# Convolution and gate columns as seven half products, and a 31-tap convolution by even and odd tokens

## The chip, the cores and the metric

The kernel runs on one core of one Trainium2 chip. The metric is the time of one execution on the device in microseconds (us), lower is better; the number that counts is the median of several executions. Beside it stands one execution taken with the hardware profiler, whose span runs from its first instruction to its last.

## The reference

One hybrid decoder block over 2048 tokens with a model width of 1024, all in float32. What the change touches is the first half of it:

```python
h = rms_norm(x, norm_w) * (1 + scale) + shift          # 2048 x 1024
z = h @ w_in                                           # one projection, 10240 columns
a, b, g_conv, q, k, v, g_attn, m_conv, m_attn = split(z)
u = a * sigmoid(b)                                     # 1024 channels
u = depthwise_causal_conv(u, conv_w, conv_b)           # 31 taps over the tokens
u = silu(layer_norm(u)) * silu(g_conv);  y_conv = u @ w_conv_out
...                                                    # attention: 12 heads in 3 dilation groups
y_attn = (o * silu(g_attn)) @ w_attn_out
y = sigmoid(m_conv) * y_conv + sigmoid(m_attn) * y_attn
out = x + gate * (y @ w_out)
```

a, b, g_conv, m_conv and m_attn are 1024 columns each of the projection: five of its ten thousand-column blocks.

## The kernel before, in words

**Number format.** Every float32 factor of a matmul is split into a high part (`hi`, `wh`: a copy by ScalarE, written ACT in the profile) and a low part (`lo`, `wl`: the factor less its high part, one subtraction on VectorE, written DVE, or on GpSimd, written POOL). A product is then three matmuls: high by high, high by low and low by high. One product of a 128-column block with 512 tokens over the 1024 rows of the model width is 8 x 3 = 24 matmuls of 128x512.

**Stages, by the time in the profiled execution.** Up to about 45 us the modulation vector, rotary tables and first loads. Then twelve units, one for each attention head (46 to 1086 us): the query, key and value columns of a head are projected for all 16 token blocks, and the blocks of the head before are attended to. During the first unit h is made (`h_first`, `h_part`): transposes on TensorE, `hf` by VectorE from PSUM (two buffers), the high part by ACT, the low part by VectorE or POOL; from then on `hT_hi` and `hT_lo` stay in SBUF, 2048 tokens each. From 1086 to 1191 us the three groups' attention is merged and multiplied by its gate (`merge_step`, two halves of the heads, 16 token blocks each, matmuls on line 350 into `pzg`). From 1193 to 2064 us runs the **channel stage**, and after it the output part: `ya` (attention output projection), the layer norm of the convolution, `yc`, and the last projection, up to the end at 2525 us.

**The channel stage.** `jobs` alternates `ab_block` and `gate_blocks` over eight blocks of 128 channels. `ab_block` computes the b column and the a column of its block for four tiles of 512 tokens (`z_chan`, 24 matmuls each on line 806), forms u with a tanh on ACT and one VectorE instruction (line 822), and puts the 31 taps of the convolution on a list (`conv_todo`): each tap is one VectorE instruction over 1024 tokens (line 835, accumulating in the SBUF tile `ca`), two of them per tap. `gate_blocks` computes three columns of a block (g_conv, m_conv, m_attn), passes them through ACT (line 864; for g_conv also line 866 on VectorE) and stores them. After each tile `run_conv` takes three to six taps from the list and issues them. Weights of the next job are loaded and split while a job runs (`load_w`, lines 316 to 329).

**What sets the order.** Within an engine's queue instructions run in the order in which they stand. TensorE's order is written out by hand in the units, the merges and the output part, and left to the framework's scheduler in the channel stage; for the other engines the scheduler decides, with a few instructions pinned. Nearly all transfers are issued by one queue, SP. A tile that is reused waits until its last reader and its last transfer are done. Before the last four tiles of the stage `beside()` calls `start_output`, which closes the convolution's pool and loads and splits w_attn_out (lines 894 to 896) in its place; the ai tiles (the attention's gated output) and the d tiles (the convolution's result, read back from DRAM) follow.

## Time and profile before

| | |
|---|---|
| median of 3 runs | 2528.01 us (2527.86 to 2530.43) |
| profiled execution | 2527.02 us, span 2525.2 us |
| granted TensorE clock, mean | 0.997 |
| TensorE (PE) busy | 2491.1 us, 99% of the span |
| VectorE (DVE) busy | 1668.0 us, 66% |
| ScalarE (ACT) busy | 756.7 us, 30% |
| GpSimd (POOL) busy | 252.7 us, 10% |
| DMA | 278.51 MB, mean 110 GB/s |

Busy times are sums over the whole span, so a share is a mean over stages with different limits; what a change in one stage is worth is read from that stage. In the groups of a view, `out<-in` are the names of the tiles that an instruction writes and reads, `x480` a count, and the time after the second bar the idle time of its engine ahead of it, with what ended that. In the timeline the first number is the start in us from the span's start and the second the duration; a row with `x2` holds two instructions. A matmul's own duration overlaps that of the next, so the pitch of TensorE's work is read from starts.

### The profile page before, as it was taken

To read this page: it belongs to the slowest core of one execution; us is meant where nothing else is said; L and a number is where in the kernel's file an instruction comes from. 1 tells how busy PE (TensorE), PEld (TensorE's weight loads), DVE (VectorE), ACT (ScalarE), POOL (GpSimd) and SP (SyncE) were. 2 spreads that over 40 slices of the span, in tenths; PEclk is the share of its full clock that TensorE was granted. 3 is DMA by queue.
4 is the path that set the end of the run, shared out by engine and by line. 5 is a ranking of instruction groups with operands and counts; after the bars stand their busy time and mean duration, and the time that the engine had idled before them with its cause. 6 is when DMAs were issued, how large, how long until landed. Compare 5 with 4: busy or idle time off the path is not lost.

```text
span 2525.2 us, 38211 instructions
## 1 busy us (share of the span) xinstructions
PE 2491.1 (99%) x13361; PEld 2222.6 (88%) x13361; DVE 1668.0 (66%) x3528; ACT 756.7 (30%) x2366; POOL 252.7 (10%) x503
## 2 busy tenths in 40 slices
...
GB/s 234 117 107 116 155 109 99 101 117 119 115 73 54 57 36 38 51 132 148 41 48 70 64 80 83 39 70 60 63 64 70 95 148 324 295 221 231 124 135 111
DMA packets 262653, 278.51 MB, mean 110 GB/s; under 512 B 25464, under 2 KB 195736, under 8 KB 262462
## 3 DMA queue, kind: packets, MB, share of 16 engines
...
HBM read 175.12 MB, written 100.86 MB: 109 GB/s over the span
## 4 chain that ended last, share of the span: by engine, by line
PE 95%; DVE 1%; ACT 1%; DMA 1%; POOL 1%; issue 0%; SPq 0%; POOLq 0%; ACTq 0%; DVEq 0%
PE pz L350 31%; PE pg L806 21%; PE yc L948 7%; PE out L948 7%; PE pb L806 7%; PE pa L806 7%; PE ya L948 3%; PE pzg L350 3%; PE ps L422 3%; PE po L441 3%; PE ptq L412 2%; PE ptp L433 1%; DMA pos_i<-in_positions_dram 0%; DVE tab L164 0%; PE pt_x L258 0%; DMA raw_u<-in_w_in_dram 0%
## 5 line engine op out<-in xcount | busy, mean ns | idle before, releaser
L835 DVE SCALAR_TENSOR_TENSOR ca<-up,chan,ca 128x1024 f32<-128x1024 f32 x480 | 593.9, 1286 | 3.6
L350 PE MATMUL pz<-wh_u,hT_lo 128*128 128x384 f32 x1536 | 536.3, 350 | 1.3 <-POOL hT_lo L271 1.2
L350 PE MATMUL pz<-wh_u,hT_hi 128*128 128x384 f32 x1536 | 518.3, 337 | 5.6 <-ACT wh_u L326 2.7
L350 PE MATMUL pz<-wl_u,hT_hi 128*128 128x384 f32 x1536 | 519.3, 338 | 0.3 <-DVE wl_u L329 0.2
L378 DVE SCALAR_TENSOR_TENSOR qk<-pz,st,wqk 128x128 f32<-128x128 f32 x384 | 117.0, 347 | 335.3 <-POOL st L107 335.3
L806 PE MATMUL pg<-hT_hi,wh_gm 128*128 128x512 f32 x768 | 298.6, 389 | 0.0
L806 PE MATMUL pg<-hT_lo,wh_gm 128*128 128x512 f32 x768 | 298.6, 389 | 0.0
L806 PE MATMUL pg<-hT_hi,wl_gm 128*128 128x512 f32 x768 | 297.9, 389 | 0.0
L350 PEld LDWEIGHTS pz<-wh_u,hT_hi 128*128 128x128 f32 x1536 | 290.5, 189 | 7.8 <-ACT wh_u L326 3.3
L350 PEld LDWEIGHTS pz<-wh_u,hT_lo 128*128 128x128 f32 x1536 | 289.2, 188 | 3.2 <-POOL hT_lo L271 1.5
L350 PEld LDWEIGHTS pz<-wl_u,hT_hi 128*128 128x128 f32 x1536 | 289.6, 189 | 2.1 <-DVE wl_u L329 1.6
L414 ACT ACTIVATE qkT<-ptq 128x256 f32<-128x256 f32 x192 | 73.8, 384 | 420.2 <-PE ptq L412 419.7
L864 ACT ACTIVATE gt<-pg 128x512 f32<-128x512 f32 x96 | 57.1, 597 | 421.4 <-PE pg L806 417.1
L806 PEld LDWEIGHTS pg<-hT_hi,wl_gm 128*128 128x128 f32 x768 | 144.2, 188 | 30.0
L806 PEld LDWEIGHTS pg<-hT_lo,wh_gm 128*128 128x128 f32 x768 | 144.2, 188 | 30.0
L806 PEld LDWEIGHTS pg<-hT_hi,wh_gm 128*128 128x128 f32 x768 | 144.2, 188 | 29.7
L107 POOL TENSOR_TENSOR st<-st,mhalf 128x2 f32<-128x2 f32 x192 | 136.5, 711 | 16.0
L367 ACT ACTIVATE sq<-pz 128x128 bf16<-128x128 f32 x384 | 106.2, 277 | 97.4 <-PE pz L350 90.3
L106 POOL TENSOR_SCALAR st<-st 128x2 f32<-128x2 f32 x192 | 45.6, 237 | 813.9 <-ACT sq L367 813.9
L427 ACT ACTIVATE sm<-sm,osb 128x128 f32<-128x128 f32 (+1 forms) x192 | 88.7, 462 | 62.3 <-DVE osb L425 59.0
L806 PE MATMUL pb<-hT_hi,wh_ab 128*128 128x512 f32 x256 | 99.7, 389 | 0.0
L806 PE MATMUL pb<-hT_lo,wh_ab 128*128 128x512 f32 x256 | 99.6, 389 | 0.0
...
## 6 DMA issues: line engine op xcount, KB each, us to landing
qkv_d<-qkv SPq DMA_DIRECT2D x128, 192.0 KB, 2.2
...
lqk<-qkv_d SPq DMA_DIRECT2D x128, 128.0 KB, 2.2
...
wada<-in_w_ada_dram SPq DMA_DIRECT2D x16, 512.0 KB, 8.2
lv<-qkv_d SPq DMA_DIRECT2D x128, 64.0 KB, 1.8
raw_ab<-in_w_in_dram SPq DMA_DIRECT2D x64, 128.0 KB, 2.2
```

The lines of the kernel that those rows point to most:

```text
L107: nc.gpsimd.tensor_tensor(dst, scratch[:, :n], mhalf[:, :n], op=ALU.pow)
L350: nc.tensor.matmul(pz[:, :width], a[:, k, P * j : P * j + P], w[:, :width], start=(m == 0), stop=(m == 23))
L367: nc.scalar.activation(sq, pz[:, P * i : P * i + P], AF.Square, scale=1.0 / math.sqrt(P), accum_out=st[:, i : i + 1])
L378: nc.vector.scalar_tensor_tensor(qk[:, 2 * i : 2 * i + 2].rearrange("p a b -> p (a b)"), pz[:, P * i : P * i + P], st[:, 2 + i : 3 + i], w ...
L414: nc.scalar.activation(qkT.rearrange("p a b -> p (a b)"), pt[:, :256], AF.Copy)
L422: nc.tensor.matmul(ps[:, P * i : P * i + P], box["q"][:, 0, :], kt[:, 1, :], start=True, stop=True)
L427: nc.scalar.activation(sm[:, :w], sm[:, :w], AF.Exp, scale=-1.0, bias=o[:, P : P + 1], accum_out=o[:, P + 1 : P + 2])
L441: nc.tensor.matmul(po[:, :P], box["pT"][:, P * i : P * i + P], vt, start=(i == 0), stop=(i == nk - 1))
L806: nc.tensor.matmul(pz, w[k][:, P * col : P * col + P], a[:, k, 512 * t : 512 * t + 512], start=(m == 0), stop=(m == 23))
L835: nc.vector.scalar_tensor_tensor(accs[c], up[:, t0 + i : t0 + i + 1024], chan[:, cb, i : i + 1], accs[c], op0=ALU.mult, op1=ALU.add)
L864: nc.scalar.activation(th, pz, AF.Tanh, scale=0.5)
L948: nc.tensor.matmul(pz, w, xx, start=(m == 0), stop=(m == len(terms) - 1))
```

## The change

**Products of halves.** The projection of the five blocks is cut in two along the tokens (two halves of 1024), the tokens of a half in two tiles of 512, the model width in two halves of 512, and the columns into pairs of 128. The two-by-two product of such quarters is done by Strassen's scheme (Winograd's form) with seven products of quarters where there were eight: `quad` runs them in the order of `PRODUCTS`, 12 matmuls each. It needs sums of quarters on both sides. Those of h (S1 to S4) are made once: h is also written to DRAM while it is made (`h_d`), VectorE forms the sums during units 4 to 10 (`quarter_load`, `quarter_sum`, kept in `s_d`), and `quarter_place` loads and splits them into the tiles of h that are no longer needed, for half 0 during the merges (whose token blocks come in another order for it), for half 1 during the last quad of half 0. Those of the weights (T1 to T4) are made per quad by POOL (`column_steps`), one quad ahead, and each of the seven weight quarters is split by ACT and by VectorE (3) or POOL (4). The sums of products run through PSUM accumulation, ACT copies (`kept`) and three additions per quad, two on VectorE and one on POOL.

**Order.** There are 40 quads, 20 per half: 8 of a and b columns, 12 of gate columns. Half 0 is done for all channels before half 1. TensorE's order is now written by hand in this stage too. After each product `after` issues one step of the next quad's weights and three or four steps of the convolution. The g_conv gate uses Silu on ACT.

**Convolution.** For each half and channel block the 31 taps are done on 512 even and 512 odd tokens: u is stored apart for even and odd tokens (`ut`), and three short filters of 16, 15 and 16 taps run over the even, the odd and the summed tokens (`both`, one POOL addition), accumulating in PSUM, with one joining step between (`conv_parts`). The last 15 values go from half 0 to half 1 by `tail` and `odd_tail`. The convolution's list is emptied before the last quad, and `start_output` stands there.

Where instructions moved, first VectorE in the middle of the channel stage. Before, in a gate block: `ca` are the two accumulators of a channel block in SBUF, `up` is u, `gt` a gate tile.

```order
L835 SCALAR_TENSOR_TENSOR ca_0_17319<-up_16743,chan,ca_0_17319 128x1024 [waits DVE_49]
L866 SCALAR_TENSOR_TENSOR gt_0_2_17120<-gt_0_2_17120,pg_0_2_17095 128x512 [waits Activation_49]
L835 SCALAR_TENSOR_TENSOR ca_1_17321<-up_16743,chan,ca_1_17321 128x1024 [waits DVE_49]
L846 TENSOR_TENSOR usum<-usum,ca_1_16651 128x1024 [waits DVE_49]
L835 SCALAR_TENSOR_TENSOR ca_0_17319<-up_16743,chan,ca_0_17319 128x1024 [waits DVE_49]
```

After, around the start of a block's convolution: `ce` is an accumulator in PSUM (L998 even tokens, L1027 the summed tokens of the block before), L919 a split of a weight quarter for the next quad, L962 and L976 additions of products, L1060 forms u. Behind them on the queue everything waits that they wait for.

```order
L976 TENSOR_TENSOR spare_hi<-spare_hi,pcab_6_18368 128x512 [waits PE_49]
L1027 SCALAR_TENSOR_TENSOR ce_5_18053<-us_5_18010,pair_taps,ce_5_18053 128x512 [waits DVE_49] x2
L1060 SCALAR_TENSOR_TENSOR ut_6_18364<-spare_hi 128x2x256 [waits Activation_49]
L1027 SCALAR_TENSOR_TENSOR ce_5_18053<-us_5_18010,pair_taps,ce_5_18053 128x512 [waits DVE_49]
L1060 SCALAR_TENSOR_TENSOR ut_6_18364<-spare_hi,paab_6_18366 128x2x256 [waits PE_49]
L919 TENSOR_TENSOR slB_896_18544<-wB_896_18535,shB_896_18543 128x512 [waits DMAHW0_49,Activation_49]
L1027 SCALAR_TENSOR_TENSOR ce_5_18053<-us_5_18010,pair_taps,ce_5_18053 128x512 [waits DVE_49]
L995 TENSOR_SCALAR ce_6_18514<-ut_6_18364,chan 128x512 [waits DVE_49]
L1027 SCALAR_TENSOR_TENSOR ce_5_18053<-us_5_18010,pair_taps,ce_5_18053 128x512 [waits DVE_49]
L998 SCALAR_TENSOR_TENSOR ce_6_18514<-ut_6_18364,chan,ce_6_18514 128x512 [waits DVE_49]
```

Fewer elements per instruction, more instructions, and the weight splits and product sums stand between the taps.

Next SP, the queue of transfers, at the end of the stage. Before, the w_attn_out loads (`fraw`, two at a time) stand among the stores of the last gate block (`gt`), ahead of all loads of ai:

```order
L867 DMA g_d<-gt_0_0_21116 128x512 [waits DMAHW3_49,DVE_49]
L894 DMA fraw<-in_w_attn_out_dram 128x512 [waits DMAHW4_49,Pool_49]
L894 DMA fraw<-in_w_attn_out_dram 128x512 [waits DMAHW5_49,PE_49]
L894 DMA fraw<-in_w_attn_out_dram 128x512 [waits DMAHW6_49,DMAHW4_49,DVE_49]
L894 DMA fraw<-in_w_attn_out_dram 128x512 [waits DMAHW7_49,DMAHW5_49,DVE_49]
L867 DMA g_d<-gt_0_1_21151 128x512 [waits DMAHW0_49,DVE_49]
```

After, behind the last store of the last quad (`gt_6`), the loads of ai, eight loads of d and the last store of the convolution; the first d waits for TensorE:

```order
L1073 DMA ma_d<-gt_6_22782 128x512 [waits DMAHW7_49,Activation_49]
L1098 DMA fraw<-ai_d 128x512 [waits DMAHW0_49]
L1098 DMA airaw<-ai_d 128x512 [waits DMAHW1_49]
L1279 DMA ma_0_22832<-ma_d 128x512 [waits DMAHW2_49]
L1187 DMA d_22841<-u_d 128x2x512 [waits DMAHW3_49,PE_49]
...
L1034 DMA u_d<-ca_7_22535 128x1024 [waits DMAHW1_49,DVE_49]
...
L1187 DMA d_23071<-u_d 128x2x512 [waits DMAHW0_49]
L1224 DMA gg_0_23350<-g_d 128x512 [waits DMAHW1_49]
...
L1098 DMA fraw<-in_w_attn_out_dram 128x512 [waits DMAHW5_49]
L1098 DMA fraw<-in_w_attn_out_dram 128x512 [waits DMAHW6_49]
```

So these loads moved from inside the stage to behind its end.

Last ACT at the change of halves: L832 takes over a placed quarter for half 1 (A or S), L955 is a `kept` copy, `paab_0` the bank of half 1's first quad, L918 a weight's high part.

```order
L832 ACTIVATE S_hi_19404<-spare_hi 128x512 [waits DMAHW3_49]
L832 ACTIVATE A_hi_19438<-landing_19447 128x512 [waits DMAHW4_49]
L832 ACTIVATE A_hi_19438<-landing_19451 128x512 [waits DMAHW5_49]
L955 ACTIVATE spare_hi<-paab_0_19457 128x512 [waits PE_49,Pool_49]
L918 ACTIVATE shT_2048_19521<-wT_2048_19519 128x512 [waits PE_49,Pool_49]
L918 ACTIVATE shT_2048_19538<-wB_2048_19473 128x512 [waits PE_49]
L955 ACTIVATE spare_hi<-paab_0_19457 128x512 [waits DVE_49,PE_49]
```

All 28 placings stand ahead of half 1's first copy out of PSUM; before, nothing of this kind was there.

The diff, cut to its core:

```diff
@@ -261,15 +276,16 @@
     def h_first(kk, pt):
         for a in range(2):
             k = 2 * kk + a
-            last = nc.scalar.activation(hi[:, k, :256], pt[:, 256 * a : 256 * a + 256], AF.Identity,
+            last = nc.scalar.activation(part(hi, k, 0, 256), pt[:, 256 * a : 256 * a + 256], AF.Identity,
                                  scale=mod[:, KC + k : KC + k + 1], bias=mod[:, k : k + 1])
         for a in range(2):
             k = 2 * kk + a
             hf = xp.tile([P, 2, 256], F32, tag="hf", name=f"hf0_{k}", bufs=2)
             nc.vector.tensor_scalar(hf[:, 0], pt[:, 256 * a : 256 * a + 256], mod[:, KC + k : KC + k + 1],
                                     mod[:, k : k + 1], op0=ALU.mult, op1=ALU.add)
-            (nc.gpsimd if a else nc.vector).tensor_tensor(lo[:, k, :256], hf[:, 0], hi[:, k, :256].bitcast(F32),
+            (nc.gpsimd if a else nc.vector).tensor_tensor(part(lo, k, 0, 256), hf[:, 0], part(hi, k, 0, 256).bitcast(F32),
                                                           op=ALU.subtract)
+            nc.sync.dma_start(h_d[k, :, :256], hf[:, 0])
...
+        nc.sync.dma_start(h_d[2 * kk : 2 * kk + 2, :, P * j : P * j + 256].rearrange("a p t -> p a t"), hf)
...
+    def quarter_sum(half, k, n, dst, x0, x1, op):
+        q = [aside["sq", name] for name in (dst, x0, x1)]
+        tc.keep_in_program_order(nc.vector.tensor_tensor(*q, op=op))
+        nc.sync.dma_start(s_d[half, n - 1, k], q[0])
...
+    PRODUCTS = (("A11", "B11"), ("A12", "B21"), ("S2", "T2"), ("S1", "T1"), ("S3", "T3"), ("S4", "B22"), ("A22", "T4"))
...
+    def quarter_place(half, name, k, cols, raw, eng):
+        if k == 0 and cols.start == 0:
+            quarter_new(half, name)
+        h, l = (x[:, k, cols] for x in quarters[name])
+        nc.sync.dma_start(raw, quarter_src(half, name, k)[:, cols])
+        nc.scalar.activation(h, raw, AF.Copy)
+        eng.tensor_tensor(l, raw, h.bitcast(F32), op=ALU.subtract)
+
+    placing = [(n, k, c) for n in ("S2", "S3", "S4", "S1") for k in range(4) for c in (0, 256)]
...
+            if half == 1 and at_j >= 8:
+                for i, (n, k, c0) in enumerate(placing[4 * (at_j - 8) : 4 * (at_j - 8) + 4]):
+                    raw = wp.tile([P, 384], F32, tag="raw", name=f"raw{n}_{k}_{c0}", bufs=3)[:, :256]
+                    quarter_place(0, n, k, slice(c0, c0 + 256), raw, nc.gpsimd if i % 2 else nc.vector)
...
+    def column_steps(c0, c1):
+
+        q, got = {}, []
+
+        def load(name, kh, c):
+            t = q[name] = wr.tile([P, 4, P], F32, tag="wr", name=f"w{name}_{c0}")
+            nc.sync.dma_start(t, w_in[512 * kh : 512 * kh + 512, c : c + P].rearrange("(k p) c -> p k c", p=P))
+
+        def combine(name, dst, x0, x1):
+            if dst is None:
+                dst = wr.tile([P, 4, P], F32, tag="wr", name=f"w{name}_{c0}")
+            nc.gpsimd.tensor_tensor(dst, x0, x1, op=ALU.subtract)
+            q[name] = dst
+
+        def split(name, eng):
+            h, l = (ws.tile([P, 4, P], F32R, tag=f"s{hl}", name=f"s{hl}{name}_{c0}") for hl in "hl")
+            nc.scalar.activation(h, q[name], AF.Copy)
+            eng.tensor_tensor(l, q[name], h.bitcast(F32), op=ALU.subtract)
+            got.append((h, l))
+
+        def step(n):
+            if n == 0:
+                load("B11", 0, c0)
+                load("B21", 1, c0)
+                load("B12", 0, c1)
+                load("B22", 1, c1)
+            if n == 2:
+                combine("T1", q["B11"], q["B12"], q["B11"])
+                combine("T2", None, q["B22"], q["T1"])
+            if n == 4:
+                combine("T3", q["B12"], q["B22"], q["B12"])
+            if n == 6:
+                combine("T4", q["B21"], q["B21"], q["T2"])
+            split(PRODUCTS[n][1], nc.vector if n in (0, 3, 5) else nc.gpsimd)
+
+        return got, [lambda n=n: step(n) for n in range(7)]
...
+    def quad(name, got, sink, after):
+
+        pa, pb, pc = bank("z", f"pa{name}"), bank("s", f"pb{name}"), bank("o", f"pc{name}")
+        first = set()
+
+        def product(n, ps, more=False):
+            ah, al = quarters[PRODUCTS[n][0]]
+            wh, wl = got.pop(0)
+            terms = [t for k in range(4) for t in ((wh[:, k], ah[:, k]), (wh[:, k], al[:, k]), (wl[:, k], ah[:, k]))]
+            for m, (w, x) in enumerate(terms):
+                nc.tensor.matmul(ps, w, x, start=(m == 0 and ps.name not in first), stop=(m == 11 and not more),
+                                 skip_group_check=True)
+            first.add(ps.name)
+
+        def kept(ps):
+            t = scratch()
+            nc.scalar.activation(t, ps, AF.Copy)
+            return t
+
+        product(0, pa, True)
+        s1 = kept(pa)
+        after(0)
+        product(1, pb)
+        nc.vector.tensor_tensor(s1, s1, pb, op=ALU.add)
+        sink(0, 0, s1)
+        after(1)
+        product(2, pa, True)
+        s2 = kept(pa)
+        after(2)
+        product(3, pc, True)
+        s5 = kept(pc)
+        after(3)
+        product(4, pa, True)
+        s3 = kept(pa)
+        nc.gpsimd.tensor_tensor(s3, s3, s5, op=ALU.add)
+        after(4)
+        product(5, pc)
+        nc.vector.tensor_tensor(s2, s2, pc, op=ALU.add)
+        sink(0, 1, s2)
+        sink(1, 1, s3)
+        after(5)
+        product(6, pa)
+        sink(1, 0, pa)
+        after(6)
...
+        def odd(j):
+            def f():
+                w = chan[:, cb, 2 * j + 1 : 2 * j + 2]
+                if j == 0:
+                    box["o"] = bank("t", f"cq{half}_{cb}")
+                    nc.vector.tensor_scalar(box["o"], o[:, 2:514], w, None, op0=ALU.mult)
+                else:
+                    psum_o = box["o"]
+                    if j == HT - 1:
+                        box["o"] = cv.tile([P, 512], F32, tag="co", name=f"co{half}_{cb}")
+                    stt(box["o"], o[:, 2 + j : 514 + j], w, psum_o, op0=ALU.mult, op1=ALU.add)
+            return f
...
+        def join():
+            y = box["y"] = cv.tile([P, 512, 2], F32, tag="ca", name=f"ca{half}_{cb}")
+            nc.vector.tensor_add(y[:, 1:, 0], box["e"][:, 1:], box["o"][:, :511])
+            if half == 0:
+                nc.vector.tensor_copy(y[:, 0:1, 0], box["e"][:, 0:1])
+                nc.vector.tensor_copy(odd_tail[:, cb : cb + 1], box["o"][:, 511:])
+            else:
+                nc.vector.tensor_add(y[:, 0:1, 0], box["e"][:, 0:1], odd_tail[:, cb : cb + 1])
+            stt(box["e"], box["e"], pair_taps[:, cb, HT + 1 : HT + 2], box["o"], op0=ALU.subtract, op1=ALU.add)
...
+        def mixed(j):
+            def f():
+                dst = box["y"][:, :, 1] if j == HT else box["e"]
+                stt(dst, both[:, 1 + j : 513 + j], pair_taps[:, cb, j : j + 1], box["e"], op0=ALU.mult,
+                    op1=ALU.subtract if j == 0 else ALU.add)
+            return f
...
+        nc.gpsimd.tensor_add(both[:, 1:], e[:, 1:], o[:, 1:])
+        if half == 0:
+            nc.gpsimd.tensor_copy(tail[:, cb], ut[:, :, 513:528])
+        return [*[even(j) for j in range(HT + 1)], *[odd(j) for j in range(HT)], join,
+                *[mixed(j) for j in range(HT + 1)], done]
...
+    got, steps = job_columns(0)
+    for f in steps:
+        f()
+    for i, (kind, half, g, cb) in enumerate(jobs):
+        last_of_half = i + 1 < len(jobs) and jobs[i + 1][1] > half
+        nxt, steps = job_columns(i + 1) if i + 1 < len(jobs) else ([], [])
+        if i + 1 == len(jobs):
+            run_conv(len(conv_todo))
+            wraw_c.__exit__(None, None, None)
+            start_output()
+
+        def after(n):
+            if steps:
+                steps[n]()
+            if last_of_half:
+                name = PRODUCTS[n][0]
+                for k in range(4):
+                    quarter_place(1, name, k, slice(0, 512), landing(4 * n + k), nc.gpsimd if k % 2 else nc.vector)
+            else:
+                run_conv(3 if n < 5 else 4)
+
+        if kind is ab_quad:
+            ab_quad(half, cb, got, after)
         else:
-            job(cb, per, wts, start_output)
+            gate_quad(half, g[1], g[2], cb, got, after)
+        got = nxt
```

213 lines of the change are left out of this document (125 added, 88 removed).

## The prediction

> **What bounds the kernel now.** I read the page's busy line and its chain of waits first, then the busy time by stretches of the span.
>
> ```profile
> PE 2491.1 (99%) x13361; PEld 2222.6 (88%) x13361; DVE 1668.0 (66%) x3528; ACT 756.7 (30%) x2366; POOL 252.7 (10%) x503
> PE 95%; DVE 1%; ACT 1%; DMA 1%; POOL 1%; issue 0%; SPq 0%; POOLq 0%; ACTq 0%; DVEq 0%
> core 0: us, PE busy (x) PEld busy (x) DVE busy (x) ACT busy (x) POOL busy (x), PEclk, DMA share, GB/s
> 140.00:1010.00 870.00, 868.49 (x5554) 862.83 (x5555) 474.18 (x1766) 340.94 (x1412) 150.15 (x324) 1.00 0.31 92
> 1215.00:2075.00 860.00, 856.23 (x3771) 707.52 (x3770) 712.19 (x704) 134.24 (x254) 0.74 (x6) 1.00 0.20 68
> 2075.00:2185.00 110.00, 110.00 (x493) 89.95 (x493) 89.28 (x145) 48.59 (x79) 3.08 (x4) 1.00 0.93 317
> ```
>
> TensorE sets the end: 95% of the chain, and in the channel stage (1215 to 2075) 856 of 860 us. VectorE is second there, 712 us of 860, and POOL does nothing (0.74 us). Right behind, in the first projection of the output part, the DMA engines are 93% busy at 317 GB/s. So fewer matmuls are worth their full time as long as VectorE, which has 17% left, keeps up, and as long as each stage hands over to the next without a pause.
>
> **The matmuls.** A stretch of the timeline gives the pitch of one 128x512 matmul (start us, us, engine, line, operation):
>
> ```profile
> 1195.06 0.39 PE L806 MATMUL pa<-hT_lo,wh_ab 128*128 128x512 f32 x1
> 1195.28 0.39 PE L806 MATMUL pb<-hT_hi,wl_ab 128*128 128x512 f32 x1
> 1195.51 0.39 PE L806 MATMUL pb<-hT_hi,wh_ab 128*128 128x512 f32 x1
> 1195.74 0.39 PE L806 MATMUL pb<-hT_lo,wh_ab 128*128 128x512 f32 x1
> ```
>
> They follow each other every 0.227 us ((1195.74 - 1195.06)/3). Before: 8 channel blocks x 5 columns x 4 token tiles x 24 matmuls = 3840. After: 40 quads x 7 products x 12 = 3360, or 762 us; a quad takes 19.05 us, a product 2.72. Gone are 480 x 0.227 = **-109 us**; the order of all other TensorE work is unchanged. -109 holds only if nothing else becomes late.
>
> **VectorE in the channel stage.** Groups by line (count | busy us, mean ns of one | idle before), and two dependent and one independent instruction from the timeline:
>
> ```profile
> L835 DVE SCALAR_TENSOR_TENSOR ca<-up,chan,ca 128x1024 f32<-128x1024 f32 x480 | 593.9, 1286 | 3.6
> L1003 DVE SCALAR_TENSOR_TENSOR vf<-d,chan,rs 128x512 f32<-128x512 f32 x32 | 23.2, 750 | 4.5 <-ACT rs L996 4.5
> L866 DVE SCALAR_TENSOR_TENSOR gt<-gt,pg 128x512 f32<-128x512 f32 x32 | 22.0, 688 | 1.8 <-ACT gt L864 1.6
> L1007 DVE SCALAR_TENSOR_TENSOR vf<-tv,gg 128x512 f32<-128x512 f32 x32 | 22.0, 689 | 3.0 <-DMA gg<-g_d 2.0 <-ACT tv L1006 0.7
> L832 DVE TENSOR_SCALAR ca<-up,chan 128x1024 f32<-128x1024 f32 x16 | 13.0, 814 | 0.5
> 2399.43 0.69 DVE L1131 TENSOR_TENSOR ot<-out,gate_row 128x512 f32<-128x512 f32 x1 [4.04 <-PE out L948]
> 2400.16 0.69 DVE L1132 TENSOR_TENSOR ot<-ot,xt 128x512 f32<-128x512 f32 x1
> 2400.77 1.22 DVE L1122 TENSOR_TENSOR yl<-yw,yh 128x1024 fp32r<-128x1024 f32 x1
> ```
>
> L835 (the 31 taps, 594 us) goes. A 128x512 step with a per-channel scalar takes 0.75 us (L1003), others 0.69. The timeline shows that an instruction begins 0.61 after one it doesn't need (2400.16 to 2400.77) and 0.73 after one whose result it reads (2399.43 to 2400.16): 0.08 less, or 0.04 more, than its own 0.69. So a tap costs 0.66, and 0.125 more where it reads its direct predecessor. In the new order I count 734 taps (240 even, 224 odd, 254 mixed, 16 at the join): 484 us, and 170 of them directly dependent: 21. Then 248 of the other 128x512 kind (120 weight splits, 80 sums of two products, 32 u, 16 joins) x 0.61 = 151; 32 first taps at half of L832's 814 ns and a bit, 14; 16 sums over 1024, about L1122's 1.15 each, 18; 24 tiny ones, 3. Together 691 us, 17.3 per quad.
>
> POOL is no longer idle: per quad 4 weight splits, 4 combinations, one sum of products, nearly one other.
>
> ```profile
> 47.24 0.73 POOL L271 TENSOR_TENSOR hT_lo<-hf,hT_hi 128x256 fp32r<-128x256 f32 x1 [2.33 <-ACT hT_hi L264]
> 40.25 1.00 POOL L329 TENSOR_TENSOR wl_u<-raw_u,wh_u 128x384 fp32r<-128x384 f32 x1 [2.13 <-ACT wh_u L326]
> 34.11 1.23 DVE L164 SCALAR_TENSOR_TENSOR tab<-na,tab 128x1024 f32<-128x1024 f32 x1
> 34.66 3.46 POOL L329 TENSOR_TENSOR wl_u<-raw_u,wh_u 128x384 fp32r<-128x384 f32 x2 [9.80 <-DMA raw_u<-in_w_in_dram]
> 35.37 1.90 DVE L164 SCALAR_TENSOR_TENSOR tab<-tab 128x1024 f32<-128x1024 f32 x1
> 37.30 1.37 DVE L165 TENSOR_SCALAR tab<-tab 128x1024 f32<-128x1024 f32 x1
> L205 DVE TENSOR_SCALAR tab<-tab 128x1024 f32<-128x1024 f32 x1 | 0.7, 694 | 0.0
> ```
>
> By the first two rows (0.73 us for 256 elements, 1.00 for 384, so 0.27 for each 128) 128x512 on POOL is an estimated 1.27 us: 9.8 x 1.27 = 12 us per quad, 62% of it. And the two engines hinder each other: while POOL splits wl_u (34.66 to 38.12), VectorE's L164, which reads two tiles of SBUF, takes 1.90 instead of 1.23 us, +0.67. L165, which reads one, takes 1.37 where its like, L205, takes 0.69: that is down to the pace per element that a tap has anyway (1.32 for 1024). So I charge only VectorE instructions with two SBUF tiles: 3.8 per quad (3 splits, part of the u's and sums); a tap has its accumulator in PSUM. At a 62% chance to meet half of a 1.27 us instruction that is 0.4 each, 61 us in all: VectorE needs 752 of TensorE's 762 us. At the rows' 0.67 for each it would be 102: 793, 31 more than TensorE. VectorE is thus at the bound, and late sums of products hold ACT, whose queue is in order and must empty a PSUM bank within one product (2.72 us). I add **+10**, nearer to the fit than to 31 (ends 0 and +31).
>
> [...]
>
> ACT has some 14 copies and activations per quad at 0.60 to 0.63 us (the first two rows below): 9 of 19 us, no bound.
>
> ```profile
> L864 ACT ACTIVATE gt<-pg 128x512 f32<-128x512 f32 x96 | 57.1, 597 | 421.4 <-PE pg L806 417.1 <-issue 4.3
> L283 ACT ACTIVATE hT_hi<-hf 128x512 fp32r<-128x512 f32 x28 | 17.5, 626 | 4.5 <-DVE hf L280 4.4
> 47.46 1.09 DVE L269 TENSOR_SCALAR hf<-pt_x,mod 128x256 f32<-128x256 f32 x2
> 48.99 1.06 DVE L269 TENSOR_SCALAR hf<-pt_x,mod 128x256 f32<-128x256 f32 x2
> raw_ab<-in_w_in_dram SPq DMA_DIRECT2D x64, 128.0 KB, 2.2
> ```
>
> **The start.** h now also goes to DRAM, so each hf tile (two of them) waits until its transfer has landed. The pairs at 47.46 and 48.99 come every 1.5 us; a 128 KB transfer lands after about 2.2 (last row above), so three rounds are each 1 to 2 us longer, and two rounds of h_part behind them too: **+6** (3 to 15), on VectorE's queue ahead of the first unit. The S sums (32 instructions, some 64 transfers) fall in units 4 to 10, where VectorE has room (474 of 870 us busy by the same table): 0.
>
> **Three hand-overs.** Transfers: KB each, median us to landing; then VectorE's splits of w_attn_out and the first matmuls of the output part.
>
> ```profile
> d<-u_d SPq DMA_DIRECT2D x16, 512.0 KB, 7.9
> fraw<-in_w_conv_out_dram SPq DMA_DIRECT2D x16, 256.0 KB, 7.1
> fraw<-ai_d SPq DMA_DIRECT2D x15, 256.0 KB, 5.0
> 2010.52 1.29 DVE L896 TENSOR_TENSOR wal<-fraw,wah 128x512 fp32r<-128x512 f32 x2 [4.76 <-ACT wah L895]
> 2024.30 0.69 DVE L896 TENSOR_TENSOR wal<-fraw,wah 128x512 fp32r<-128x512 f32 x1 [0.90 <-ACT wah L895]
> 2065.30 0.50 PE L948 MATMUL ya<-ai_0h,wah 128*128 128x512 f32 x1 [1.25 <-ACT ai_0h L895]
> ```
>
> Merges to stage: the first quad's weights need a chain of POOL combinations and splits (T1, T2, its split: three of 1.27 us, plus ACT) before its third product, and the space of their tiles comes free only with the old pools. Two or three us late at several places: **+6** (3 to 12).
>
> Half 0 to half 1: 28 tiles of 256 KB are placed while the last quad runs; with 8 weight loads and its results that is some 11 MB, at the 317 GB/s of the table 35 us from that quad's start, against its 19. ACT's first copy of half 1 stands behind all of them, so the third product, due at 24.5, waits until 35: **+10** (4 to 15; nothing hides it, since TensorE's order is fixed).
>
> Stage to output: the w_attn_out splits were done at 2024.99, 40 us ahead of the first ya at 2065.30. Now SP issues those loads behind 8 d loads of 512 KB, the last u_d store and 15 others, about 6.8 MB (21 us at 317 GB/s), and they go two at a time through a ring, four rounds of 5 to 7 us, the first of them inside the 21. ya_0 needs all eight. 21 + 3 x 6 = 39, less 3 that the first loads gain while the last product runs: **+36** (20 to 45). What was in those transfers' way before, the first ya stage at 93% DMA, gets emptier in exchange, but TensorE had no wait there to give back.
>
> **Sum.** Profiled time 2527.02 (span 2525.2, 1.8 around it): 2527 - 109 + 10 + 6 + 6 + 10 + 36 = **2486**. The median of the runs, 2528.01, is 1 us above the profile's time, within their spread (2527.86 to 2530.43).
>
> **Rivals.** (a) Hand-overs mostly hidden and VectorE keeps up: 2527 - 109 + 20 = 2438. For it: SP issues ahead, and 317 GB/s may not be the limit of short queues; against: the order of the loads. 0.22. [...] 0.15. (c) **Slower:** VectorE becomes the bound since the taps accumulate in PSUM, and no VectorE row of before writes PSUM. If every tap, also one that doesn't follow its own predecessor, pays the 0.125 of a dependent one: 564 x 0.125 = 71 us, VectorE 823, 51 above the 772 in my sum: 2537. [...] Against it: reading PSUM costs no time (L866, which reads it, 688 ns; L1007, which doesn't, 689). 0.11. [...]
>
> **Chances and range.** My forecast 0.52, with its own range 2462 to 2512. The range of 8 in 10 has to take in (a) nearly, (b), and (c): 2436 to 2540. What this kernel's runs can tell from no change is 0.2%, 5 us. Faster than that: the forecast, (a), most of (b): 0.84; slower: (c) and tails, 0.11; the rest, where hand-overs and port cost happen to eat the 109 just about, 0.05.
>
> **What would show it.** A stage of 762 to 775 us from first to last quad product, with VectorE over 95% busy; sums of products waiting for VectorE rather than for TensorE; a 128x512 tap near 0.75 us (above 0.83: rival c); TensorE idle about 10 us at the change of halves on ACT's copy, and about 36 us before the first ya blocks on wal. Wrong would be: a quad above 20 us (VectorE is the bound), or ya starting within 10 us (the loads don't wait as read).

## The result and the profile after

The changed kernel takes 2502.42 us (median of 4 runs, 2498.76 to 2504.48), the kernel before 2528.02 us in the same session (4 runs, 2527.86 to 2530.43). The ratio is 0.9895, with a 95% interval from 0.9878 to 0.9912: 25.6 us are gained where 42 were forecast. The time lies inside the range given (2436 to 2540) and inside the forecast's own range (2462 to 2512).

The page of the changed kernel answers the busy line and the chain of waits shown of before:

```profile
PE 2400.5 (96%) x12881; PEld 2140.7 (86%) x12881; DVE 1747.3 (70%) x3945; ACT 971.0 (39%) x2738; POOL 799.2 (32%) x925
PE 81%; DVE 8%; DMA 5%; ACT 2%; issue 2%; POOL 1%; SPq 0%; DVEq 0%; ACTq 0%; POOLq 0%
```

480 matmuls are gone (13361 to 12881). TensorE now makes up 81% of the chain instead of 95%; VectorE, transfers and ACT have taken the rest. The profiled execution has a span of 2500.7 us (2525.2 before). From the starts of the first and last matmul of each stage, that difference is:

| piece of the span, us | before | after | difference | predicted |
|---|---|---|---|---|
| up to the first matmul of the merges (`pzg`) | 1086.5 | 1091.8 | +5.3 | +6 |
| from there to the first matmul of the channel stage | 106.9 | 117.0 | +10.1 | +6, with the first quad |
| first to last matmul of the channel stage | 870.3 | 790.0 | -80.3 | -109 + 10 + 10 |
| last matmul of the stage to the last `ya` | 98.2 | 137.2 | +39.0 | +36 |
| from there to the end | 363.3 | 364.7 | +1.4 | 0 |

The waits of TensorE by what released them (us in total, times, longest) name the places:

```profile
PE ya L1171 <- ACT wah L1099: 38.7, 4, 27.9
PE paab L949 <- ACT spare_hi L955: 11.9, 1, 11.9
PE pta L517 <- POOL sg L512: 8.4, 8, 2.4
PE pag_ma_d L949 <- ACT spare_lo L955: 4.6, 1, 4.6
PE paab L949 <- POOL slT L919: 1.8, 1, 1.8
```

Before, two of these places had rows of the same kind:

```profile
PE pta L500 <- POOL sg L495: 2.7, 3, 1.6
PE ya L948 <- ACT ai_2h L895: 1.5, 1, 1.5
```

After, the first row is the start of the output part, the second and fourth are the change of halves (16.5 us), the third the merges, the fifth the first quad. Sums of products that are late in the steady run of quads hardly show: two rows of 0.5 and 0.3 us in all. The same by stretches: the start of the stage, half 0, a stretch around the change of halves, half 1 in its steady part, and the start of the output part.

```profile
core 0: us, PE busy (x) PEld busy (x) DVE busy (x) ACT busy (x) POOL busy (x), PEclk, DMA share, GB/s
1190.00:1215.00 25.00, 20.94 (x125) 18.86 (x126) 13.03 (x41) 13.82 (x39) 14.44 (x19) 0.86 0.58 174
1215.00:1600.00 385.00, 377.80 (x1644) 310.46 (x1644) 370.85 (x524) 166.48 (x298) 269.50 (x213) 0.99 0.34 107
1600.00:1622.00 22.00, 10.11 (x44) 8.04 (x44) 19.85 (x22) 13.02 (x24) 18.73 (x14) 0.76 0.71 219
1640.00:1990.00 350.00, 350.00 (x1545) 289.40 (x1544) 343.57 (x494) 145.02 (x258) 227.06 (x175) 1.00 0.30 94
2000.00:2050.00 50.00, 12.12 (x29) 7.98 (x30) 23.57 (x35) 18.03 (x29) 0.00 (x0) 0.56 0.86 290
```

In the 350 us from 1640 TensorE is busy throughout with VectorE at 98%: the two just fit. The PEclk column (the granted clock) shows something that the stretches of before, all at 1.00, did not: 0.56, 0.76 and 0.86 where TensorE waited. A stretch of TensorE's timeline at the change of halves shows what this does to the matmuls:

```profile
1621.40 0.80 PE L949 MATMUL paab<-S_hi,shT 128*128 128x512 f32 x1 [11.89 <-ACT spare_hi L955]
1622.00 0.63 PE L949 MATMUL paab<-S_lo,shT 128*128 128x512 f32 x1
1622.42 0.63 PE L949 MATMUL paab<-S_hi,slT 128*128 128x512 f32 x1
...
1625.37 0.39 PE L949 MATMUL paab<-S_hi,shT 128*128 128x512 f32 x1
1625.59 0.39 PE L949 MATMUL paab<-S_lo,shT 128*128 128x512 f32 x1
```

Behind the wait the matmuls come every 0.43 us, for some 4 us (the granted clock is 0.50 from 1621.5 to 1625), then every 0.23 again. Over the stage, 41 matmuls at the slow pitch cost 7.3 us, and the five steps with a wait in them 19.9; together 27.2 of the 28 us that the stage's 790.0 lie above 3360 x 0.227 = 762.

### The profile page after: what moved, and what is told of

Its sections match the earlier page's. It is cut to its first block, busy times and chain, and to the rows that moved or that the text cites. A ratio compares the mean times of both kernels' runs of the same rounds, so it can differ in the third digit from the quotient of the medians.

```text
span 2500.7 us, 39106 instructions
## 1 busy us (share of the span) xinstructions
PE 2400.5 (96%) x12881; PEld 2140.7 (86%) x12881; DVE 1747.3 (70%) x3945; ACT 971.0 (39%) x2738; POOL 799.2 (32%) x925
## 4 chain that ended last, share of the span: by engine, by line
PE 81%; DVE 8%; DMA 5%; ACT 2%; issue 2%; POOL 1%; SPq 0%; DVEq 0%; ACTq 0%; POOLq 0%
PE pz L367 29%; PE out L1171 7%; PE yc L1171 7%; PE paab L949 6%; PE ya L1171 4%; PE pag_g_d L949 3%; PE pcab L949 3%; PE pag_mc_d L949 3%; PE ps L439 3%; PE po L458 3%; PE pag_ma_d L949 2%; PE ptq L429 2%; PE pcg_g_d L949 2%; PE pcg_mc_d L949 1%; PE pbab L949 1%
## 5 line engine op out<-in xcount | busy, mean ns | idle before, releaser
L395 DVE SCALAR_TENSOR_TENSOR qk<-pz,st,wqk 128x128 f32<-128x128 f32 x384 | 117.0, 346 | 317.9 <-POOL st L111 317.7
L1027 DVE SCALAR_TENSOR_TENSOR ce<-us,pair_taps,ce 128x512 f32<-128x512 f32 x240 | 179.3, 747 | 2.3
L998 DVE SCALAR_TENSOR_TENSOR ce<-ut,chan,ce 128x512 f32<-128x512 f32 x240 | 178.4, 743 | 0.0
L1011 DVE SCALAR_TENSOR_TENSOR cq<-ut,chan,cq 128x512 f32<-128x512 f32 x208 | 155.7, 748 | 2.7
L919 POOL TENSOR_TENSOR slT<-wB,shT 128x512 fp32r<-128x512 f32 x80 | 112.1, 1402 | 62.9 <-ACT shT L918 62.6
L913 POOL TENSOR_TENSOR wB<-wB,wB 128x512 f32<-128x512 f32 x80 | 107.7, 1346 | 72.4 <-DVE slB L919 66.6
L918 ACT ACTIVATE shB<-wB 128x512 fp32r<-128x512 f32 x120 | 75.3, 628 | 120.2 <-issue 93.3
L1354 DVE TENSOR_TENSOR ot<-out,gate_row 128x512 f32<-128x512 f32 x32 | 22.1, 692 | 116.2 <-PE out L1171 116.2
L458 PE MATMUL po<-lv,pT 128*128 128x128 f32 x600 | 97.2, 273 | 0.0
L918 ACT ACTIVATE shT<-wB 128x512 fp32r<-128x512 f32 x120 | 74.7, 623 | 56.7 <-PE pcab L949 18.3
L458 PEld LDWEIGHTS po<-lv,pT 128*128 128x128 f32 x600 | 93.1, 189 | 0.5 <-issue 0.5
```

The source lines that it names most:

```text
L395: nc.vector.scalar_tensor_tensor(qk[:, 2 * i : 2 * i + 2].rearrange("p a b -> p (a b)"), pz[:, P * i : P * i + P], st[:, 2 + i : 3 + i], w ...
L458: nc.tensor.matmul(po[:, :P], box["pT"][:, P * i : P * i + P], vt, start=(i == 0), stop=(i == nk - 1))
L913: nc.gpsimd.tensor_tensor(dst, x0, x1, op=ALU.subtract)
L918: nc.scalar.activation(h, q[name], AF.Copy)
L919: eng.tensor_tensor(l, q[name], h.bitcast(F32), op=ALU.subtract)
L998: stt(box["e"], e[:, 1 + j : 513 + j], chan[:, cb, 2 * j : 2 * j + 1], box["e"], op0=ALU.mult, op1=ALU.add)
```

## The experiments

The question was where 16 us of the forecast went, and whether the terms that came out right did so for the reasons given. Where a kernel ran once, its time stands against 2502.48 us, the profiled execution of the changed kernel; those that ran several times have a range. Single runs also differ where the edit changes nothing. In the changed kernel and in the five one-run experiments that touch nothing ahead of the stage and its first weights (loads first, with and without the wider ring, landing tiles, half the bytes, accumulators in SBUF), the stage's first matmul stands between 1208.0 and 1211.7. So a difference of some 4 us in a single total tells nothing, and the pieces of the span are compared.

### The end: loads of w_attn_out first

```diff
-                split(wh[k][:, sl], wl[k][:, sl], w_attn_out[...])
+                big["last"] = split(wh[k][:, sl], wl[k][:, sl], w_attn_out[...])
...
+              with tc.issue_after(big["last"].ins):
                 nc.sync.dma_start(self.d[:, 2 * i ...      # and likewise later ai, gg, w_conv_out
```

> The changed kernel, with the order of SP's queue alone changed at the end of the channel stage: the d, later ai, gg and w_conv_out loads are queued behind the w_attn_out loads. Theory (the 38.7 us in which TensorE waits for wah in the first ya block are time in which the w_attn_out loads stand behind the d loads in SP's queue, and then go two at a time): the loads start right behind the convolution's last store at about 2007 us, four rounds of some 4 us, and the second ya block starts near 2024 us instead of 2044.3: about 20 us less, total near 2482. Rival (the loads are held by the DMA engines' bandwidth, or by the memory of the convolution that their tiles take over, not by their place in the queue): the second ya block stays at 2040 or later, total 2497 to 2502.

Measured: 2486.87 us, 15.6 less; the first `ya` starts at 2014.4 instead of 2027.1, and its waits are

```profile
PE ya L1172 <- ACT wah L1099: 21.6, 4, 13.9
```

instead of 38.7. The time from the stage's last matmul to the last `ya` falls from 137.2 to 120.2 us, so 17 of the 39 us were the place of these loads on SP's queue behind the d loads. The second `ya` block, for which the theory had 2024 and the rival 2040 or later, starts at 2028.4. Of the changed kernel SP's timeline (start us, duration) shows that place:

```profile
2001.74 2.32 SPq L1187 DMA_DIRECT2D d<-u_d  x4
...
2011.97 2.93 SPq L1187 DMA_DIRECT2D d<-u_d  x4
2015.78 1.66 SPq L1224 DMA_DIRECT2D gg<-g_d  x3
2017.84 0.32 SPq L1098 DMA_DIRECT2D fraw<-ai_d  x1
2019.15 1.69 SPq L1098 DMA_DIRECT2D fraw<-in_w_attn_out_dram  x2
```

The first load of w_attn_out is issued at 2019.15, 20 us behind the stage's last matmul (1998.8), and the first `ya` starts at 2027.1, 28 us behind it. The prediction had 21 us with the first round of loads inside them, so the place in the queue cost more than reckoned; the three rounds behind it took less, 15.7 us up to the last wait's end at 2042.8, where 18 were reckoned.

Does the ring of two landing tiles hold what is left? Every second load was given a tile of the gate pool, five in flight, on top of the edit above:

```diff
+                                    raw=gp.tile([P, 512], F32, tag="gt", name="wraw") if c0 else None)
```

> As the run before, and every second w_attn_out load lands in one of the three gate tiles, so that five loads are under way instead of two. Theory (place in the queue and the two-tile ring): three loads already land before the stage ends, the rest in one or two rounds; second ya block near 2016 us, total near 2474. Rival (the split tiles take over memory of the convolution's last block, which is stored only at 2008 us, and that sets the start): no earlier than without the wider ring, near 2024, total 2482.

Measured: 2484.48 us. The ring gives 2.4 us of the 8 that the theory gave it (2482 to 2474), less than single runs differ by; the first `ya` starts at 2014.1, as without it (2014.4). So the rival has it: something else sets the start. A row of VectorE and one of the waits of SP's queue name it:

```profile
2012.54 1.90 DVE L1100 TENSOR_TENSOR wal<-wraw,wah 128x512 fp32r<-128x512 f32 x3 [1.86 <-DMA u_d<-ca]
SPq L1034 <- DVE ca L1027: 6.2, 1, 6.2
```

The low part of w_attn_out is written where the convolution's tiles were, and waits for the store of the last of them. SP, whose queue runs in order, waits 6.2 us for the convolution's last tap before it can issue that store (2009.45), and only then issues the next two loads of w_attn_out (2009.81); the first `ya` waits for the copy of one of these (ACT `wah`, 2013.40 to 2014.03). By both ways the end of the convolution now sets the start of the output part; the first `ya` itself waits by the way through SP's queue.

### The change of halves: ACT's order, bytes, or the engines

First, ACT's copy out of PSUM (`kept`) was let past the last four placings: the last fourteen use five landing tiles instead of seven, so that the two scratch tiles which the copies need are free early:

```diff
-        if i % 7 < 4:
-            return scratch(i % 7)
+        if i < 14:
+            if i % 7 < 4:
+                return scratch(i % 7)
+        elif (i - 14) % 5 < 2:
+            return scratch(2 + (i - 14) % 5)
```

> The changed kernel, with the last 14 of the 28 landing tiles at the change of halves taken from two scratch tiles and the three gate tiles instead of four and three, so that the two scratch tiles which the first quad of half 1 needs first are free early, and its first copies out of PSUM stand ahead of the last placings in ACT's queue (the first by four). Theory (TensorE's 11.9 us wait at 1621 us is the copy's place behind all placings on ACT): the first copy comes about 8 us earlier and the wait shrinks to about 4, but later products wait for their quarters, 2 to 4 us in all; total 2494 to 2498. Rival (the placings' transfers alone set the pace, and the third product would wait for its quarter anyway): the waits between 1590 and 1640 stay at 16.5 us in sum, total 2500 to 2504; fewer landing tiles could add to that.

Measured: 2501.17 us. The waits at the change are 4.84 + 1.93 + 5.91 = 12.7 us instead of 16.5: the copy comes earlier, and later products wait instead. That lies between the theory (6 to 8) and the rival (16.5). The stage is 3.0 us shorter (787.0), which a start 2.6 us later hides in the total. ACT's order, with the tiles given up for it, is worth about 4 us; it is where the wait shows, but not what sets most of it.

Then the transfers: each placing of half 1 loads half the bytes and uses them twice, so that half 1 computes with other numbers; the number of instructions on ACT, VectorE and POOL is the same.

```diff
+        if half == 1:
+            nc.sync.dma_start(raw[:, :256], quarter_src(half, name, k)[:, :256])
+            two = raw[:, None, :256].to_broadcast([P, 2, 256])
...
```

> The changed kernel, with each of the 28 placings at the change of halves loading only the first 256 of its 512 columns and using them twice (so half 1's products are of other numbers): the same instructions of the same size, 3.7 MB less transferred. Theory (the bytes set the pace of the change of halves): the waits there, 16.5 us, fall to 4 to 8, and with them the slow clock behind them; total 2486 to 2494. Rival (the ring of seven landing tiles, SP's order and ACT's queue set it, each transfer's fixed time counting more than its bytes): waits of 12 us or more, total 2497 to 2503.

Measured: 2496.0 us, the waits 1.91 + 11.90 = 13.8 us: half of the placings' bytes take away 2.7 of 16.5. The waits are the rival's (12 or more); the total lies between the two forecasts, 6.5 us lower, of which the stage holds 3.4 and the rest lies ahead of it and behind it. Busy time in the 40 us around the change (columns as above), first in the changed kernel, then in this experiment:

```profile
1578.00:1618.00 40.00, 26.90 (x109) 21.39 (x107) 36.96 (x44) 23.84 (x43) 34.66 (x24) 0.84 0.78 238
```

```profile
1578.00:1618.00 40.00, 26.11 (x105) 20.55 (x104) 39.75 (x46) 25.57 (x47) 38.19 (x26) 0.87 0.54 165
```

The DMA share falls from 0.78 to 0.54, and now VectorE and POOL are both busy nearly throughout: 39.75 and 38.19 of 40 us. Some of their instructions are also slower than elsewhere; both engines read two SBUF tiles for a placing. VectorE's placings take 0.95 to 1.38 us by groups (L833), where a split that nothing holds up takes 0.69, and POOL's rows in the changed kernel are:

```profile
1588.15 1.28 POOL L913 TENSOR_TENSOR wB<-wB,wT 128x512 f32<-128x512 f32 x1
1589.39 1.72 POOL L833 TENSOR_TENSOR A_lo<-spare_hi,A_hi 128x512 fp32r<-128x512 f32 x1
1591.07 1.26 POOL L919 TENSOR_TENSOR slT<-wT,shT 128x512 fp32r<-128x512 f32 x1
1592.29 1.72 POOL L833 TENSOR_TENSOR A_lo<-landing,A_hi 128x512 fp32r<-128x512 f32 x1
```

The same shape takes 1.28 us or 1.72. The prediction let the third product of half 1 start 35 us behind the start of the last quad of half 0, from bytes over GB/s. It starts 43.5 us behind it (1577.9 to 1621.4) in the changed kernel and 40.7 here, though by that sum 3.7 MB less at 317 GB/s should have given 11.6 us. So bytes are the smaller part of it. The last experiment below tests the hindrance between VectorE and POOL; the number of transfers and of landing tiles is the same here, and what a transfer costs apart from its bytes was not varied.

### The price of a tap, and where the accumulator is

The accumulators of the short filters were put in SBUF, in tiles of the same size:

```diff
-                    box["e"] = bank("t", f"ce{half}_{cb}")
+                    box["e"] = cv.tile([P, 512], F32, tag="ce", name=f"ce{half}_{cb}", bufs=2)
...
-                    box["o"] = bank("t", f"cq{half}_{cb}")
+                    box["o"] = cv.tile([P, 512], F32, tag="co", name=f"co{half}_{cb}")
...
```

> The changed kernel, with the accumulators of the short filters in SBUF instead of PSUM; the instructions and their order stay. Each tap then reads two tiles of SBUF, as L164 does in the profile of before. Theory (VectorE instructions with two SBUF tiles and POOL instructions exclude each other, and the taps escape that by their accumulator in PSUM): 734 taps pay 0.3 to 0.6 us more each, VectorE becomes the bound, the stage grows from 790 to between 980 and 1150 us, total 2690 to 2860, and POOL's 128x512 instructions go from 1.3 us to over 1.6. [...]

Measured: 2787.53 us, 285 us slower. Groups of VectorE by line in the stage (count | busy us, mean ns | idle before), first the changed kernel, then this one:

```profile
L998 DVE SCALAR_TENSOR_TENSOR ce<-ut,chan,ce 128x512 f32<-128x512 f32 x240 | 178.4, 743 | 0.0
L1027 DVE SCALAR_TENSOR_TENSOR ce<-us,pair_taps,ce 128x512 f32<-128x512 f32 x237 | 177.1, 747 | 2.2
L1011 DVE SCALAR_TENSOR_TENSOR cq<-ut,chan,cq 128x512 f32<-128x512 f32 x208 | 155.7, 748 | 2.7
L919 DVE TENSOR_TENSOR slB<-wB,shB 128x512 fp32r<-128x512 f32 x79 | 70.5, 892 | 4.9 <-ACT shB L918 4.3 <-DMA wB<-in_w_in_dram 0.5
L919 DVE TENSOR_TENSOR slT<-wB,shT 128x512 fp32r<-128x512 f32 x40 | 54.9, 1372 | 14.7 <-ACT shT L918 8.6 <-POOL wB L913 5.9
```

```profile
L998 DVE SCALAR_TENSOR_TENSOR ce<-ut,chan,ce 128x512 f32<-128x512 f32 x219 | 258.8, 1182 | 0.0
```

With one operand in PSUM a tap takes 743 to 748 ns, the same as L1003 with two tiles of SBUF and POOL idle (750). With both in SBUF, beside a busy POOL, it takes 1182, and POOL's splits go from 1402 ns to

```profile
L919 POOL TENSOR_TENSOR slT<-wB,shT 128x512 fp32r<-128x512 f32 x80 | 135.7, 1696 | 103.4 <-ACT shT L918 94.1 <-issue 7.9 <-PE paab L949 1.3
```

The stage is then 1086.5 us long. Rival (c) of the prediction is refuted: PSUM costs a tap nothing. And the placing of the accumulator, which the prediction only used to say which instructions are charged, decides whether this change gains or loses.

Nor do the products help without the short filters. Here the old convolution, 31 taps of 128x1024 in SBUF, stands in the new stage:

```diff
-        return [*[even(j) for j in range(HT + 1)], *[odd(j) for j in range(HT)], join,
-                *[mixed(j) for j in range(HT + 1)], done]
+        return [*[tap(i) for i in range(TAPS)], done]
...
-                run_conv(3 if n < 5 else 4)
+                run_conv(2)
```

> One part of the change alone: the seven products stay, the convolution is done as before, 31 taps of 128x1024 per half and channel block, accumulating in SBUF (496 taps), with no POOL addition for it. Theory (the seven products can gain only if the convolution leaves VectorE free and its taps don't read two SBUF tiles beside POOL): without contention VectorE needs 496 x 1.2 + 170 + 45 = about 810 us, with 0.4 per tap for POOL some 1010: the stage takes 950 to 1080 us, total 2660 to 2800, slower than before. Rival (the old taps would do): 810 to 840 us, total 2520 to 2550.

Measured: 2812.91 us, a little above the theory's 2660 to 2800. The taps, 1286 ns before, now take

```profile
L996 DVE SCALAR_TENSOR_TENSOR ca<-ut,chan,ca 128x1024 f32<-128x1024 f32 x469 | 823.6, 1793 | 1.0
```

beside a POOL that makes and splits weights, and the stage takes 1084.0 us. The products need the short filters. The filters without the products were not run; with TensorE busy in 856 of 860 us of the stage before, they would have had little to give.

### How near VectorE is to the bound

One more weight split per quad was given to VectorE, one fewer to POOL:

```diff
-            split(PRODUCTS[n][1], nc.vector if n in (0, 3, 5) else nc.gpsimd)
+            split(PRODUCTS[n][1], nc.vector if n in (0, 2, 3, 5) else nc.gpsimd)
```

> The changed kernel, with four weight splits per quad on VectorE and three on POOL, instead of three and four: 40 x 0.6 to 1.0 us more for VectorE, 24 to 40 us. Theory (VectorE stands just below the bound, with some 20 us of room in the 762 us of matmuls): it becomes the bound by a little, the stage grows by 5 to 25 us and TensorE waits for ACT's copies or for weights in most quads; total 2508 to 2527. Rival (VectorE has room to spare; its 96% busy time is made up of work that isn't waited for): the stage stays at 790 us, total 2500 to 2505.

Measured: 2512.33 us, 9.9 more, but 3.9 of them lie ahead of the stage, where single runs differ by as much. The quads hardly stretched: the stage takes 791.2 us (790.0). Inside it the waits for ACT's copies in the quads of half 0 rise from 0.8 to 5.2 us, but the first quad's wait for POOL (1.8) and 1.7 us of the slow clock fall away; in half 1 TensorE is busy throughout, as before. What came later was the output part: from the stage's last matmul to the last `ya` it is 4.8 us longer (142.0), TensorE waits 44.0 us there (38.7), and the first `ya` starts at 2038.0 instead of 2027.1. The last sum of the convolution on VectorE, first in the changed kernel, then here, is 20 us later:

```profile
2006.85 1.22 DVE L1038 TENSOR_TENSOR usum<-usum,ca 128x1024 f32<-128x1024 f32 x1
```

```profile
2026.78 1.22 DVE L1038 TENSOR_TENSOR usum<-usum,ca 128x1024 f32<-128x1024 f32 x1
```

So a late VectorE holds up the products by little (some 4 us), since their sums stand between the taps; what it holds up is the end of the list of taps, and through that the output part. The rival has the stage's length, the theory a part of its waits; the total is in the theory's range, but only some 6 of the 9.9 us can be the edit's.

### The merges and the start

All placings of half 0 on VectorE, none on POOL:

```diff
-                    quarter_place(0, n, k, slice(c0, c0 + 256), raw, nc.gpsimd if i % 2 else nc.vector)
+                    quarter_place(0, n, k, slice(c0, c0 + 256), raw, nc.vector)
```

> The changed kernel, with all 32 placings of half 0 during the merges subtracted by VectorE instead of every second one by POOL. Theory (the merges are 10 us longer than before because POOL's placings stand in its queue ahead of the products sg that TensorE's transposes wait for, and because TensorE's clock falls after each such wait): the waits of pta for sg fall from 8.4 us to 2 or 3, the merges from 117 to 110 to 113 us, total 2495 to 2499. Rival (VectorE's and ACT's placings, or the transfers of the parts, delay the merges as much): merges stay at 116 us or more, total 2501 to 2506.

Measured: 2504.2 us, the merges 120.1 us (117.0), and the waits for the gate on POOL (`sg`) no smaller:

```profile
PE pta L517 <- POOL sg L512: 12.3, 10, 3.3
```

The theory falls: POOL's queue isn't what makes `sg` late. And three hf tiles instead of two:

```diff
-            hf = xp.tile([P, 2, 256], F32, tag="hf", name=f"hf0_{k}", bufs=2)
+            hf = xp.tile([P, 2, 256], F32, tag="hf", name=f"hf0_{k}", bufs=3)
...
-        hf = xp.tile([P, 2, 256], F32, tag="hf", name=f"hf{j}_{kk}", bufs=2)
+        hf = xp.tile([P, 2, 256], F32, tag="hf", name=f"hf{j}_{kk}", bufs=3)
```

> The changed kernel, with three hf tiles instead of two. Theory (the first unit is 5.3 us late because hf tiles wait for their transfer to DRAM): one transfer more may be under way, the first merge matmul comes 2 to 4 us earlier than 1091.8, total 2497 to 2500. Rival (the transfers themselves, 8 MB beside the first units' loads, delay weights and x on SP's queue): no earlier than 1091, total 2501 to 2504.

Measured: 2501.11 us, `pzg` at 1092.8 (1091.8) where the theory had 2 to 4 us earlier. In the other single runs, with no edit there, it lies between 1090.0 and 1094.3, so a gain of 2 us could hide; nothing shows that the number of tiles costs the start its 5 us, although the size was forecast right.

### Versions that beat both

With the loads of w_attn_out first and their wider ring, the landing tiles as in the experiment above, and the placings of half 0 spread over twelve blocks of the merges instead of eight:

```diff
-            if half == 1 and at_j >= 8:
-                for i, (n, k, c0) in enumerate(placing[4 * (at_j - 8) : 4 * (at_j - 8) + 4]):
+            if half == 1 and at_j >= 4:
+                for i, (n, k, c0) in enumerate(placing[8 * (at_j - 4) // 3 : 8 * (at_j - 3) // 3]):
```

> Four edits of the changed kernel together: w_attn_out loads ahead of the d loads, a ring of five tiles for them, the two scratch tiles freed early at the change of halves, and the 32 placings of half 0 spread over twelve token blocks of the merges instead of eight. Theory (the edits fall in different places and add): 2502 less 20 (seen with the first two), less 2, and less 3 to 6 from the merges if their density delays them: 2474 to 2481. Rival (the merges are as long, since each placing delays what follows it by the same amount wherever it is): 2480 to 2485, merges still 117 us or more.

Measured: 2482.41 us (2479.72 to 2483.47), ratio to the kernel before 0.9813 (0.9798 to 0.9827). The merges took 119.0 us: spreading the placings gives nothing, as the rival has it. Then, in the order of the quads, one gate quad later:

```diff
-            for _ in range((1, 1, 2, 1, 1, 2, 1, 3)[cb]):
+            for _ in range((1, 1, 2, 1, 1, 1, 1, 4)[cb]):
```

> As the kernel with four edits, and one gate quad moved from ahead of the last two channel blocks to behind them in each half, so that the last convolution starts one quad (19 us) earlier. Theory (what is left of the wait for wah is the convolution's tail on VectorE, 10 us behind TensorE): the tail ends 5 to 12 us earlier and the first ya blocks with it; 2466 to 2475. Rival (VectorE has no room to do the convolution earlier; what is gained at the end is lost as waits in the quads ahead): 2476 to 2484.

Measured: 2478.51 us (2476.49 to 2479.25), ratio 0.9797 (0.9781 to 0.9813). The convolution's last sum comes 3.0 us earlier (2004.2 instead of 2007.2) and the first `ya` 3.4 (2008.4 instead of 2011.8). So the theory has the direction, with less than its 5 to 12 us, and the time falls in the rival's range; what the rival gave as the reason, waits in the quads ahead, doesn't show, since the stage is shorter (786.2 us, 789.1 in the run before).

Last, the theory left for the change of halves: that VectorE and POOL hold each other up there (POOL's 1.72 us for 1.28, above). On top of the last version, all placings of the change go to VectorE:

```diff
-                    quarter_place(1, name, k, slice(0, 512), landing(4 * n + k), nc.gpsimd if k % 2 else nc.vector)
+                    quarter_place(1, name, k, slice(0, 512), landing(4 * n + k), nc.vector)
```

> The kernel with four edits (loads of w_attn_out first, the larger ring of landing tiles, placings spread over twelve blocks, the order of halves with one change) and, as the one new edit, all placings of halves at the change subtracted by VectorE and none by POOL. [...] POOL was busy in 37.7 of its 44 us there, at 1.72 instead of 1.28 us for a subtraction, and VectorE in 39.5 of 44. [...] TensorE's waits there, 11.4 us without this edit (4.34 + 2.28 + 4.83), fall to 5 or less, and the time, 2478.5 without it, to 2470 to 2474. Rival: the landing tiles and the order of the loads on SP set it. The waits stay at 10 us or more and the time at 2476 to 2481.

Measured: 2479.27 us (2475.12 to 2481.14), ratio 0.9797 (0.9784 to 0.9811): the same time. Inside, the theory shows in part, and what shows doesn't pay. The waits at the change fall from 11.4 to 7.1 us (3.7 + 3.4), not to the 5 or less that it asked for, and the stage shortens from 786.2 to 780.3 us. But the time from the stage's last matmul to the last `ya` grows from 115.2 to 122.7. VectorE at the end of the stage, first without this edit, then with it:

```profile
2004.21 1.22 DVE L1041 TENSOR_TENSOR usum<-usum,ca 128x1024 f32<-128x1024 f32 x1
2006.84 1.90 DVE L1103 TENSOR_TENSOR wal<-wraw,wah 128x512 fp32r<-128x512 f32 x3 [1.41 <-DMA u_d<-ca]
```

```profile
2005.60 1.23 DVE L1041 TENSOR_TENSOR usum<-usum,ca 128x1024 f32<-128x1024 f32 x1
2008.62 1.90 DVE L1103 TENSOR_TENSOR wal<-wraw,wah 128x512 fp32r<-128x512 f32 x3 [1.79 <-DMA u_d<-ca]
```

The convolution's last sum (L1041) comes 1.4 us later, since VectorE has 14 more instructions, and w_attn_out's split behind it 1.8 later; that TensorE was done 5.7 us earlier (1991.4 instead of 1997.1) only makes it wait longer. So once the loads are first, by these two runs, VectorE sets when the output part starts, and a wait of TensorE inside the stage, as long as VectorE works through it, costs nothing more. The rival's time was met, though not its waits of 10 us or more: 4.3 us went with the landing tiles and SP's queue unchanged.

## Why the prediction was right, step by step, and where its sizes were off

**Matmuls, -109: right.** The pitch stayed at 0.227 us, and no other TensorE work changed. The sign named for it, a stage of 762 to 775 us, was too narrow for the prediction's own sum: 870.3 - 109 + 10 + 10 is 781, and 790.0 was measured.

**VectorE's load: right.** A tap takes 743 to 748 ns, and the timeline gives the steps of 0.66 and, for a direct successor, 0.78 that the sum used (for 734 taps; the trace has 736, which is 1.3 us more):

```profile
1399.47 0.74 DVE L998 SCALAR_TENSOR_TENSOR ce<-ut,chan,ce 128x512 f32<-128x512 f32 x1
1400.13 0.74 DVE L1011 SCALAR_TENSOR_TENSOR cq<-ut,chan,cq 128x512 f32<-128x512 f32 x1
1400.91 0.75 DVE L1011 SCALAR_TENSOR_TENSOR co<-ut,chan,cq 128x512 f32<-128x512 f32 x1
```

The price of POOL beside VectorE was charged to the right instructions: the splits took 892 and 1372 ns instead of 690, which is 79 x 0.202 + 40 x 0.682 = 43 us, and the sums over 1024 (1589 ns on average, 1.22 us without POOL) some 5 more: 48 of the 61 us reckoned. The 343.57 us in 350 are 18.7 per quad; predicted were 752/40 = 18.8. Rival (b) of the chances, the full 0.67 us on each of these instructions (VectorE at 793 us), is refuted; so is (c), whose mark of 0.83 us a tap is 0.75 and 83 ns, (41 + 20)/734, at which the 41 us forecast as gained and VectorE's 20 us of room (772 less 752) would be used up. What the chances call port cost is the surcharge of the splits; that a port is behind it no run shows, only that instructions of the two engines wait for each other (last section).

**Coupling of VectorE to ACT and TensorE, "+10": failed in size.** It was about 1 us: with 98% on VectorE, TensorE had no gap from 1640 to 1990. The step behind it, "late sums of products hold ACT", hardly happened: the sums stand between the taps in VectorE's queue, and what comes late is the list of taps. The experiment with a fourth split shows where such lateness goes: some 4 us into the quads, and 20 us to the end of the list, for which the output part then waits.

**Half 0 to half 1, "+10": failed in size, and its mechanism in part.** Waits of 16.5 us, and 4 to 5 more at the slow clock. The place was right, the third product of half 1 waiting for ACT's copy behind the placings. The cause given, 11 MB at 317 GB/s, was not: half of the placings' bytes took away 2.7 us. With POOL's fourteen subtractions moved, 4.3 of 11.4 us went. What the remaining 7 us hang on isn't settled; the number of transfers and the place of their loads in SP's queue were not varied.

**Merges to stage, "+6": too small.** The first quad's wait for POOL's split (slT, 1.8 us) is as told, but 10.1 us came ahead of it: waits for `sg` went from 2.7 to 8.4 (5.7), shB cost 1.2, and the slow clock behind the longest of these waits 1.7; 1.5 are left. Behind the first matmul the slow clock took another 3. Two guesses at the cause, POOL's placings and their density, gave nothing. Why `sg` is late stays open.

**Start, +6: the size right (5.3), the reason not shown.** A third hf tile brought no gain that shows, so the wait for the tile is hardly it; whether the transfers to DRAM themselves are, wasn't tried.

**Stage to output, +36: right (39.0).** The loads' place behind the d loads gave 17 of it in the experiment. In the changed kernel the end of the convolution (its last sum ends at 2008.1) was hidden behind those loads. Within the term the first round of loads was some 7 us later than reckoned and the three behind it 2 us faster.

So the two terms of 10 us were wrong in opposite ways, about 9 less in the steady quads and about 11 more at the change of halves, and some 9 more went around the merges and the first quad. That the first two nearly cancel is luck, and part of why the total came this close. Of the 16 us between 2486 and 2502.5, 3 are in the end and 1.4 in what follows it; some 2 stay unassigned. Rival (a), hand-overs mostly hidden, had 20 us lost in all where 84.5 were (109 less the 24.5 of the span).
